# Weights' low parts kept in DRAM between token blocks, and a memset between GpSimd's scatters

## The chip, the cores and the metric

One core of one Trainium2 chip runs the whole program. The metric is the device time of one execution in microseconds (us), lower is better; the number shown is the median over runs.

## The reference

One layer of a streaming encoder on 1024 tokens of 1024 channels, all in float32:

```python
n = modulate(rms_norm(h, g_norm1[l]), shift1, scale1)
p = n @ w_in[l]
a_val, a_gate, u, v, gate_a, gate_b = jnp.split(p, splits, axis=-1)
y_a = conv_branch(a_val, a_gate, ...)          # GLU, causal depthwise conv of width 31, LayerNorm, silu, @ w_conv_out
y_b = sgu_branch(u, v, ...)                    # LayerNorm, masked 128x128 mixing per group, @ w_sgu_out
merged = jax.nn.sigmoid(gate_a) * y_a + jax.nn.sigmoid(gate_b) * y_b
h = h + gate1[:, None, :] * (merged @ w_out[l])

n2 = modulate(rms_norm(h, g_norm2[l]), shift2, scale2)
h = h + gate2[:, None, :] * peer(n2, w_query[l], sub_keys[l], expert_u[l], expert_v[l])
return rms_norm(h, g_final)
```

`peer` is a retrieval: for each token and each of 8 heads the scores against 2 x 128 keys, the 16 best pairs, and a softmax over them, which gives 128 experts of 16384 with a gate each. An expert is one row of `expert_u` (dot product with the token, gelu, times the gate) and one row of `expert_v` (added with that factor).

## The kernel before, in words

The work has two parts, the front (everything up to the scores and the choice of experts) and the dense stage (the experts).

The front takes the tokens in three blocks of 3, 2 and 3 tiles of 128 tokens (`BLOCKS`). Each block multiplies the same 88 weight tiles of 128x1024: 8 each of `w_v`, `w_av`, `w_ag`, `w_u`, `w_gb`, `w_sgu`, `w_ga`, `w_conv`, `w_out`, and 16 of `w_q`; `w_v`, `w_av` and `w_ag` of the next block come while the present block does `w_q`. A float32 product is made of three faster ones (`mm3`): weights and inputs are each split into a high part, a rounded copy (`whi`, by ScalarE, line 203), and a low part, the difference (`wlo`, by VectorE, line 161). `fetch_w` loads the next raw tile (two buffers), `split_w` starts the split as a task, `next_w` hands out a finished pair and starts another, so two pairs are under way ahead of the one in use.

The order of all instructions on each engine is laid down when the program is built, by a planner (`Plan`) that adds up assumed costs and gives background work its turn: routing and convolution first, then the rest. Loads and most stores go through SyncE's queue (SP) in program order; a transfer at its head that waits holds up those behind it.

Routing (`route`, on VectorE) chooses the experts of one tile after another. What follows depends on the tile. For tiles 0 to 2 the gates are added into an array `g_a` in DRAM, which was filled with zeros at the start: per tile 128 indirect DMAs issued by GpSimd (`scatter`, line 573), each with one gate for each of the 128 tokens, at the places that a tile `at` names (line 1234). The 16 of a head wait for those of the head before. For tiles 3 and 4 the gates are expanded by one-hot products (`Scatter`): VectorE makes `o1`, `o2` and `so`, PE multiplies, ScalarE gathers 32 tokens in four `st` tiles (`evacuate`) and these are stored to `g_b`. For tiles 5 to 7 the numbers of the experts are stored.

The last block's last two scores are stored by GpSimd (`store` with `late`), behind what GpSimd has in its queue. `fence`, a memset of one column on GpSimd, waits for all scatters; the loads of the gates from `g_a` wait for the fence. The dense stage then runs all experts over tiles 0 to 4 on PE (`u_piece`, `v_unit`) with these gates, while GpSimd gathers single experts' rows for tiles 5 to 7 (line 1396) and VectorE multiplies them.

Of the kernel before, what the change touches and what calls it, by code (L numbers as in the profile page):

```python
# [7 lines left out]
F32 = mybir.dt.float32  # L8
F32R = mybir.dt.float32r
# [7 lines left out]
P = 128  # L17
D = 1024
# [14 lines left out]
TC = 32  # L33
NCH = NB // TC
ZW, ZN = 128, 16
NST = 5
NRAW = 2
NSO = 2
NPG = 3
# [262 lines left out]
def build(ctx, tc, I, O):  # L302
    nc = tc.nc
    out = O["out"]
    pl = Plan(nc)
    ctx.enter_context(tc.manual_schedule())

    dram = ctx.enter_context(tc.tile_pool(name="dram", bufs=1, space=bass.MemoryType.DRAM))
# [6 lines left out]
    g_a = dram.tile([NCA, P, P * TC], F32, name="g_a")  # L315
    g_b = dram.tile([NCH - NCA, P, P * TC], F32, name="g_b")
    g_1 = g_a.rearrange("c p (x o) -> (c p x) o", o=1)
    e_d = dram.tile([NA, P, P], I32, name="e_d")
    ga_d = dram.tile([NA, P, P], F32, name="ga_d")

    cst = ctx.enter_context(tc.tile_pool(name="cst", bufs=1))
# [126 lines left out]
    class Scatter:  # L448
# [50 lines left out]
        def produce(self):  # L499
            n, last = 0, None  # L500
            while n < NOH * self.NQ or last:
                if last:
                    while len(self.so) > 1:
                        yield pl.now + 0.2
                    r = yield from self.scaled(*last)
                    self.so.append(r)
                    last = None
                    if n % self.NQ == 0:
                        self.tiles.pop(0)
                if self.tiles:  # L510
                    last = yield from self.onehots(n)
                    n += 1
                    self.made = n
                else:
                    yield pl.now + 0.3
# [32 lines left out]

    SYNC = mybir.DependencyInfo(mybir.DependencyClass.Sync, mybir.DependencyReason.DATA)
    zeroed, heads = [], []  # L550

    def zeros(zt):

# [8 lines left out]
    def scatter(gate, at):  # L562


        while not zeroed:
            yield pl.now + 2.0
        yield max(pl.ready(at), pl.ready(gate))
        before = []
        for h in range(H):
            now = []  # L570
            for k in range(h * K, (h + 1) * K):
                nc.gpsimd.nop()
                i = nc.gpsimd.indirect_dma_start(  # L573
                    out=g_1, out_offset=bass.IndirectOffsetOnAxis(ap=at[:, k:k + 1], axis=0),
                    in_=gate[:, k:k + 1], in_offset=None, compute_op=OP.add).ins
                tc.declare_no_dep(i, group="sc", keep=before, reason="other tokens, or other experts")
                for o in before:
                    tc.add_manual_dep(i, o.name, SYNC, reason="sums of gates")
                tc.add_to_no_dep_group("sc", i)
                pl.op("pool", 2.0, [], [gate, at])  # L580
                now.append(i)
            before = now
            yield max(pl.now, pl.t["pool"] - 30.0)
        heads.append(before)
# [32 lines left out]
    def flat(w):  # L617
        return w.rearrange("p j c -> p (j c)")

    def weights():  # L620
        def w_v():
            for cb in range(2):
                for jq in range(4):
                    yield flat(I["w_v"][cb, jq])

        yield from w_v()
        for b in range(len(BLOCKS)):
            for j in range(J):
                if b == 0:
                    yield flat(I["w_av"][j])  # L630
                    yield flat(I["w_ag"][j])
                yield flat(I["w_u"][j])
            for j in range(J):
                yield flat(I["w_gb"][j])
                yield flat(I["w_sgu"][j])
            for n in ("w_ga", "w_conv"):
                for j in range(J):
                    yield flat(I[n][j])
            for cb in range(2):
                for jq in range(4):  # L640
                    yield flat(I["w_out"][cb, jq])
            if b + 1 < len(BLOCKS):
                yield from w_v()
            for j in range(J):
                if b + 1 < len(BLOCKS):
                    yield flat(I["w_av"][j])
                    yield flat(I["w_ag"][j])
                yield flat(I["w_q"][2 * j])
                yield flat(I["w_q"][2 * j + 1])

    wsrc = weights()
    raws, ahead = [], []

    def fetch_w():
        src = next(wsrc, None)
        if src is not None:
            raws.append(wp.tile([P, D], F32, name="raw", tag="raw", bufs=2))
            pl.load(raws[-1], src)

    def split_w():  # L660
        if raws:
            hi = wp.tile([P, D], F32R, name="whi", tag="whi", bufs=3)
            lo = wp.tile([P, D], F32R, name="wlo", tag="wlo", bufs=3)
            raw = raws.pop(0)

            def work():
                yield from pl.split(hi, lo, raw)
                fetch_w()

            ahead.append((hi, lo, pl.task(work())))  # L670
            ahead[-1][2][3] = -1
# [1023 lines left out]
```

## Time and profile before

| | |
|---|---|
| median of 3 runs | 3475.64 us (3469.93 to 3485.93) |
| profiled execution | 3466.49 us, of which the span is 3464.4 |
| granted TensorE clock, mean | 0.946 |
| PE busy | 3094.6 us (89%) |
| VectorE (DVE) busy | 2999.9 us (87%) |
| ScalarE (ACT) busy | 1142.6 us (33%) |
| GpSimd (POOL) busy | 1683.9 us (49%) |

The span runs from the first to the last instruction of the profiled execution. Busy times are sums over stages that differ: in the front (about the first 1500 us) and in the dense stage (from about 1640 us) other engines can set the pace, so the stages are to be read one by one.

### The profile page before, as it was taken

The numbers are of one execution on the slowest core, as the hardware profiler recorded it, in microseconds if no ns is written. First come the engines' busy times: TensorE is split into PE (matmuls) and PEld (weight loads), VectorE is DVE, ScalarE is ACT, GpSimd is POOL, SyncE is SP. The second block draws the span as 40 slices with busy tenths as digits, with TensorE's granted clock in tenths as the row PEclk, the third lists the DMA queues.
The fourth block names the chain that finished last, engine by engine and source line by source line (L and its number), as shares of the span: only waits on it lengthen the run. The fifth ranks groups of instructions, "written<-read, shape, count | busy, mean of one in ns | idle before, by whom it ended". The sixth has DMA issues, their size and how long they took to land.

```text
span 3464.4 us, 48530 instructions
## 1 busy us (share of the span) xinstructions
PE 3094.6 (89%) x17598; PEld 2811.1 (81%) x17598; DVE 2999.9 (87%) x5922; ACT 1142.6 (33%) x1964; POOL 1683.9 (49%) x1165
## 2 busy tenths in 40 slices
PE   7978969977989978954999999999999999999991
PEld 4977848966889967954999998888899998999991
DVE  3898768988999987745999998999999998999998
ACT  4324434435442335631322222222222223222221
POOL 0000000037788888883222555666665554655664
PEclk9989979998999988977999999999999999999995
DMA  5965655546655547653766899999999998999997
GB/s 190 278 208 164 214 180 171 171 125 153 162 127 122 122 89 179 160 144 81 235 217 216 305 353 331 363 333 370 341 357 346 349 347 304 357 346 361 341 347 287
DMA packets 434721, 852.71 MB, mean 246 GB/s; under 512 B 83272, under 2 KB 242888, under 8 KB 434480
## 3 DMA queue, kind: packets, MB, share of 16 engines
q1 hardware_dynamic: 268464, 446.28, 38.3%
q0 software_dynamic: 166016, 403.32, 36.5%
q8 instruction: 138, 2.26, 0.3%
q14 instruction: 103, 0.84, 0.1%
HBM read 785.94 MB, written 63.52 MB: 245 GB/s over the span
## 4 chain that ended last, share of the span: by engine, by line
PE 34%; DVE 27%; DMA 14%; POOL 12%; issue 9%; ACT 2%; SPq 0%; DVEq 0%; POOLq 0%; ACTq 0%
PE pa L144 13%; POOL g_a L573 10%; PE ps L144 9%; PE pk L144 7%; PE pr L144 5%; DMA w<-in_v,e 4%; DVE wlo L161 4%; DVE ya L174 4%; DMA raw<-in_v 4%; DVE zc L174 3%; DVE odd L174 3%; DVE scr L174 2%; POOL w L1396 1%; DMA w<-in_u,e 1%; DVE yb L161 1%
## 5 line engine op out<-in xcount | busy, mean ns | idle before, releaser
L573 POOL DMA_INDIRECT g_a<-gate,at x384 | 706.7, 1840 | 883.4 <-DVE at L168 744.2
L1396 POOL DMA_INDIRECT w<-in_u,e x384 | 483.2, 1258 | 541.6 <-DVE scr L174 367.8
L144 PE MATMUL pa<-n2h,uh 128*128 128x320 f32 x2016 | 624.9, 310 | 82.2 <-ACT ge L195 75.1
L1396 POOL DMA_INDIRECT w<-in_v,e x384 | 489.7, 1275 | 336.8 <-DVE ya L174 238.0
L144 PE MATMUL pa<-n2l,uh 128*128 128x320 f32 x2016 | 625.6, 310 | 0.2 <-DVE n2l L161 0.2
L144 PE MATMUL pa<-n2h,ul 128*128 128x320 f32 x2016 | 625.0, 310 | 0.0
L174 DVE SCALAR_TENSOR_TENSOR ya<-w,aa,ya 128x1024 f32<-128x1024 f32 x381 | 488.9, 1283 | 23.8 <-DMA w<-in_v,e 19.1
L174 DVE SCALAR_TENSOR_TENSOR scr<-w,n 128x1024 bf16<-128x1024 f32 x384 | 469.1, 1222 | 10.2 <-DMA w<-in_u,e 4.8
L144 PEld LDWEIGHTS pa<-n2h,uh 128*128 128x128 f32 x2016 | 380.5, 189 | 94.4 <-ACT ge L195 77.9
L203 ACT CAST whi<-raw 128x1024 fp32r<-128x1024 f32 x264 | 276.4, 1048 | 370.3 <-PE ps L144 100.9
L144 PEld LDWEIGHTS pa<-n2l,uh 128*128 128x128 f32 x2016 | 380.1, 189 | 10.9 <-DVE n2l L161 1.1
L161 DVE TENSOR_TENSOR wlo<-raw,whi 128x1024 fp32r<-128x1024 f32 x264 | 320.9, 1219 | 75.1 <-ACT whi L203 73.1
L144 PE MATMUL ps<-nh,whi 128*128 128x384 f32 (+1 forms) x1024 | 355.9, 348 | 31.5 <-DVE z L161 17.5
L144 PEld LDWEIGHTS pa<-n2h,ul 128*128 128x128 f32 x2016 | 380.5, 189 | 0.0
L144 PE MATMUL ps<-nh,wlo 128*128 128x384 f32 (+1 forms) x1024 | 345.8, 338 | 21.9 <-DVE wlo L161 21.8
L144 PE MATMUL ps<-nl,whi 128*128 128x384 f32 (+1 forms) x1024 | 344.7, 337 | 1.6 <-DVE nl L161 1.6
L195 ACT ACTIVATE ge<-pa 128x320 f32<-128x320 f32 x249 | 108.5, 436 | 693.6 <-PE pa L144 693.6
L144 PE MATMUL pk<-vh,hh 128*128 128x512 f32 x768 | 299.5, 390 | 0.0
L144 PE MATMUL pk<-vl,hh 128*128 128x512 f32 x768 | 299.5, 390 | 0.0
L144 PE MATMUL pk<-vh,hl 128*128 128x512 f32 x768 | 299.3, 390 | 0.0
L203 ACT CAST hh<-ge 128x320 fp32r<-128x320 f32 x250 | 115.0, 460 | 526.5 <-DVE ge L161 526.5
L144 PE MATMUL ps<-gh,whi 128*128 128x256 f32 (+1 forms) x704 | 218.3, 310 | 20.3 <-ACT gh L203 18.4
(251 smaller groups left out, 6538.3 us busy)
## 6 DMA issues: line engine op xcount, KB each, us to landing
raw<-in_uT SPq DMA_DIRECT2D x128, 512.0 KB, 6.6
raw<-in_v SPq DMA_DIRECT2D x128, 512.0 KB, 7.3
g_a<-zt SPq DMA_DIRECT2D x24, 1024.0 KB, 6.9
raw<-in_w_q SPq DMA_DIRECT2D x48, 512.0 KB, 3.9
gt<-g_a SPq DMA_DIRECT2D x32, 640.0 KB, 14.6
aw<-in_w_ada SPq DMA_DIRECT2D x32, 512.0 KB, 7.3
g_b<-st SPq DMA_DIRECT2D x32, 512.0 KB, 4.1
gt<-g_b SPq DMA_DIRECT2D x32, 512.0 KB, 12.5
```

The costliest lines, as they stand in the source:

```text
L144: self.nc.tensor.matmul(ps, w, x, start=start, stop=stop)
L161: self.nc.vector.tensor_tensor(out=out, in0=a, in1=b, op=op)
L174: self.nc.vector.scalar_tensor_tensor(out, a, s, b, op0=op0, op1=op1, **kw)
L195: self.nc.scalar.activation(out, a, func, **kw)
L203: self.nc.scalar.copy(out, a)
L573: i = nc.gpsimd.indirect_dma_start(out=g_1, out_offset=bass.IndirectOffsetOnAxis(ap=at[:, k:k + 1], axis=0), in_=gate[:, k:k + 1], in_offs ...
L1396: nc.gpsimd.indirect_dma_start(out=w, out_offset=None, in_=I["v" if ph else "u"], in_offset=bass.IndirectOffsetOnAxis(ap=ra[a][0][:, k:k + ...
```

## The change

Three things change. First, when block 0 has split a weight tile, its low part is also stored to a DRAM tile of its own (`lo_d`); when a later block comes to a tile that has one, the low part is loaded (`fetch_lo`, one tile ahead) and VectorE's subtraction is left out. The high part is still copied from the raw tile. `wlo` gets a fourth buffer. Second, space for it is taken from `st`: four buffers instead of five, and `produce` makes the next `so` when none is waiting instead of at most one. Third, between two scatters GpSimd runs a memset of one column of a tile `pad` in place of a nop, and the planner counts 1.9 us for a scatter instead of 2.0.

```diff
--- before.py
+++ after.py
@@ -33,7 +33,7 @@
 TC = 32
 NCH = NB // TC
 ZW, ZN = 128, 16
-NST = 5
+NST = 4
 NRAW = 2
 NSO = 2
 NPG = 3
@@ -315,6 +315,7 @@
     g_a = dram.tile([NCA, P, P * TC], F32, name="g_a")
     g_b = dram.tile([NCH - NCA, P, P * TC], F32, name="g_b")
     g_1 = g_a.rearrange("c p (x o) -> (c p x) o", o=1)
+    lo_d = {}
     e_d = dram.tile([NA, P, P], I32, name="e_d")
     ga_d = dram.tile([NA, P, P], F32, name="ga_d")
 
@@ -500,7 +501,7 @@
             n, last = 0, None
             while n < NOH * self.NQ or last:
                 if last:
-                    while len(self.so) > 1:
+                    while self.so:
                         yield pl.now + 0.2
                     r = yield from self.scaled(*last)
                     self.so.append(r)
@@ -548,6 +549,7 @@
 
     SYNC = mybir.DependencyInfo(mybir.DependencyClass.Sync, mybir.DependencyReason.DATA)
     zeroed, heads = [], []
+    pad = cst.tile([P, 1], F32, name="pad")
 
     def zeros(zt):
 
@@ -569,7 +571,7 @@
         for h in range(H):
             now = []
             for k in range(h * K, (h + 1) * K):
-                nc.gpsimd.nop()
+                nc.gpsimd.memset(pad, 0.0)
                 i = nc.gpsimd.indirect_dma_start(
                     out=g_1, out_offset=bass.IndirectOffsetOnAxis(ap=at[:, k:k + 1], axis=0),
                     in_=gate[:, k:k + 1], in_offset=None, compute_op=OP.add).ins
@@ -577,7 +579,7 @@
                 for o in before:
                     tc.add_manual_dep(i, o.name, SYNC, reason="sums of gates")
                 tc.add_to_no_dep_group("sc", i)
-                pl.op("pool", 2.0, [], [gate, at])
+                pl.op("pool", 1.9, [], [gate, at])
                 now.append(i)
             before = now
             yield max(pl.now, pl.t["pool"] - 30.0)
@@ -621,51 +623,69 @@
         def w_v():
             for cb in range(2):
                 for jq in range(4):
-                    yield flat(I["w_v"][cb, jq])
+                    yield "w_v", (cb, jq)
 
         yield from w_v()
         for b in range(len(BLOCKS)):
             for j in range(J):
                 if b == 0:
-                    yield flat(I["w_av"][j])
-                    yield flat(I["w_ag"][j])
-                yield flat(I["w_u"][j])
+                    yield "w_av", (j)
+                    yield "w_ag", (j)
+                yield "w_u", (j)
             for j in range(J):
-                yield flat(I["w_gb"][j])
-                yield flat(I["w_sgu"][j])
+                yield "w_gb", (j)
+                yield "w_sgu", (j)
             for n in ("w_ga", "w_conv"):
                 for j in range(J):
-                    yield flat(I[n][j])
+                    yield n, (j)
             for cb in range(2):
                 for jq in range(4):
-                    yield flat(I["w_out"][cb, jq])
+                    yield "w_out", (cb, jq)
             if b + 1 < len(BLOCKS):
                 yield from w_v()
             for j in range(J):
                 if b + 1 < len(BLOCKS):
-                    yield flat(I["w_av"][j])
-                    yield flat(I["w_ag"][j])
-                yield flat(I["w_q"][2 * j])
-                yield flat(I["w_q"][2 * j + 1])
+                    yield "w_av", (j)
+                    yield "w_ag", (j)
+                yield "w_q", (2 * j)
+                yield "w_q", (2 * j + 1)
 
     wsrc = weights()
-    raws, ahead = [], []
+    raws, ahead, los = [], [], {}
 
     def fetch_w():
-        src = next(wsrc, None)
-        if src is not None:
-            raws.append(wp.tile([P, D], F32, name="raw", tag="raw", bufs=2))
-            pl.load(raws[-1], src)
+        k = next(wsrc, None)
+        if k is not None:
+            raws.append((k, wp.tile([P, D], F32, name="raw", tag="raw", bufs=2)))
+            pl.load(raws[-1][1], flat(I[k[0]][k[1]]))
+
+    def fetch_lo():
+
+        if raws and raws[0][0] in lo_d:
+            k = raws[0][0]
+            los[k] = wp.tile([P, D], F32R, name="wlo", tag="wlo", bufs=4)
+            pl.load(los[k].bitcast(F32), lo_d[k])
 
     def split_w():
         if raws:
             hi = wp.tile([P, D], F32R, name="whi", tag="whi", bufs=3)
-            lo = wp.tile([P, D], F32R, name="wlo", tag="wlo", bufs=3)
-            raw = raws.pop(0)
+            k, raw = raws.pop(0)
+            old = k in los
+            lo = los.pop(k) if old else wp.tile([P, D], F32R, name="wlo", tag="wlo", bufs=4)
 
             def work():
+                if old:
+                    yield pl.ready(raw)
+                    f = pl.acopy(hi, raw)
+                    fetch_w()
+                    fetch_lo()
+                    yield max(f, pl.ready(lo))
+                    return
                 yield from pl.split(hi, lo, raw)
                 fetch_w()
+                lo_d[k] = dram.tile([P, D], F32, name="lo_d_%s_%s" % (k[0], str(k[1]).strip("()").replace(", ", "_")))
+                pl.load(lo_d[k], lo.bitcast(F32))
+                fetch_lo()
 
             ahead.append((hi, lo, pl.task(work())))
             ahead[-1][2][3] = -1
```

## Rows read from the trace of the kernel before

**Rows 1.** The page of the profiled execution: busy time, share and instructions of each engine, and then the span in 40 slices of 86.6 us, each digit the busy share in tenths.

```profile
PE 3094.6 (89%) x17598; PEld 2811.1 (81%) x17598; DVE 2999.9 (87%) x5922; ACT 1142.6 (33%) x1964; POOL 1683.9 (49%) x1165
...
PE   7978969977989978954999999999999999999991
...
POOL 0000000037788888883222555666665554655664
```

**Rows 2.** The page's chain of work that ended last: its share of the span by line.

```profile
PE pa L144 13%; POOL g_a L573 10%; PE ps L144 9%; PE pk L144 7%; PE pr L144 5%; DMA w<-in_v,e 4%; DVE wlo L161 4%; DVE ya L174 4%; DMA raw<-in_v 4%; DVE zc L174 3%; DVE odd L174 3%; DVE scr L174 2%; POOL w L1396 1%; DMA w<-in_u,e 1%; DVE yb L161 1%
```

**Rows 3.** The chain of waits between 1400 and 1660 us, all engines: engine, line, whom it waited for, us in total, times, longest.

```profile
ACT vh L203 <- DMA sc_d<-so: 72.3, 1, 72.3
...
PE pa L144 <- ACT ge L195: 71.8, 1, 71.8
```

**Rows 4.** The waits of SyncE's DMA queue between 1480 and 1660 us, same columns.

```profile
SPq L236 <- DVE vals L355: 78.3, 4, 71.7
```

**Rows 5.** The timeline of GpSimd from 1586 to 1600 us: start, us, engine, line, operation, and in brackets the idle time before it.

```profile
1591.62 1.55 POOL L573 DMA_INDIRECT g_a<-gate,at  x1 [0.30 <-issue]
1592.60 2.23 POOL L229 DMA_DIRECT2D sc_d<-so  x2
1594.79 0.16 POOL L589 MEMSET fence<- 128x1 f32 x1
```

**Rows 6.** The waits of GpSimd over 600 to 1800 us.

```profile
POOL g_a L573 <- DVE at L168: 744.2, 1, 744.2
POOL g_a L573 <- issue: 113.6, 373, 0.3
...
POOL g_a L573 <- DMA g_a<-gate,at: 24.9, 8, 6.4
```

**Rows 7.** The instructions that write or read the tile at (the scatters' places) between 600 and 1100 us: count, duration in ns (smallest, median, largest), first and last start.

```profile
L573 POOL DMA_INDIRECT g_a<-gate,at x149: 1544/1569/9207, 747.3 to 1099.7; - x149
L168 DVE TENSOR_SCALAR at<-i1f,tok x3: 286/286/286, 746.7 to 1029.2; 128x128 int32<-128x128 f32 x3
```

**Rows 8.** GpSimd's scatters as one group, first in 747 to 1532 us and then in 1532 to 1600 us (two answers): count, busy us and mean ns of one, idle time before them and who ended it.

```profile
L573 POOL DMA_INDIRECT g_a<-gate,at x352 | 657.0, 1866 | 869.1 <-DVE at L168 744.2 <-issue 104.5 <-DMA g_a<-gate,at 19.8
...
L573 POOL DMA_INDIRECT g_a<-gate,at x32 | 49.8, 1555 | 14.2 <-issue 9.1 <-DMA g_a<-gate,at 5.1
```

**Rows 9.** GpSimd's timeline from 800 to 812 us, a scatter over a subtraction.

```profile
801.23 1.56 POOL L573 DMA_INDIRECT g_a<-gate,at  x1 [0.31 <-issue]
803.09 2.78 POOL L573 DMA_INDIRECT g_a<-gate,at  x1 [0.30 <-issue]
```

**Rows 10.** VectorE's timeline in the same place.

```profile
803.22 1.22 DVE L161 TENSOR_TENSOR wlo<-raw,whi 128x1024 fp32r<-128x1024 f32 x1
```

**Rows 11.** Busy time by stretch. Columns: stretch, its length, PE, PEld, DVE, ACT, POOL busy us with counts, granted clock, DMA share, GB/s.

```profile
87.00:174.00 87.00, 84.82 (x500) 84.18 (x499) 74.87 (x137) 28.96 (x37) 0.00 (x0) 1.00 0.91 278
...
478.00:642.00 164.00, 152.21 (x972) 145.11 (x971) 138.07 (x318) 71.34 (x121) 0.00 (x0) 0.98 0.55 182
642.00:747.00 105.00, 95.67 (x775) 92.88 (x774) 96.06 (x282) 40.66 (x59) 0.00 (x0) 1.00 0.50 158
747.00:1500.00 753.00, 654.51 (x3869) 597.63 (x3868) 656.81 (x1781) 344.94 (x688) 632.35 (x337) 0.92 0.59 138
1500.00:1593.00 93.00, 20.68 (x122) 18.32 (x119) 20.08 (x65) 14.32 (x32) 74.20 (x49) 0.61 0.43 84
...
1641.00:3464.00 1823.00, 1741.77 (x9733) 1581.84 (x9731) 1695.20 (x2696) 479.24 (x782) 972.95 (x768) 0.98 0.91 324
```

**Rows 12.** All instructions that write or read the tile wlo: count, duration in ns (smallest, median, largest), first and last start.

```profile
L161 DVE TENSOR_TENSOR wlo<-raw,whi x264: 1203/1219/1273, 42.9 to 1471.4; 128x1024 fp32r<-128x1024 f32 x132
```

**Rows 13.** Busy time by stretch of the instructions that write or read the tile wlo alone: stretch, length, PE, PEld, DVE busy us with counts, granted clock, DMA share, GB/s.

```profile
87.00:174.00 87.00, 51.52 (x154) 28.76 (x153) 23.19 (x19) 1.00 0.91 278
478.00:642.00 164.00, 88.62 (x277) 53.02 (x277) 46.27 (x38) 0.98 0.55 182
642.00:747.00 105.00, 67.03 (x237) 44.41 (x237) 35.30 (x29) 1.00 0.50 158
747.00:1500.00 753.00, 309.68 (x908) 176.28 (x908) 146.79 (x121) 0.92 0.59 138
```

**Rows 14.** VectorE's costliest groups between 747 and 1500 us.

```profile
L161 DVE TENSOR_TENSOR wlo<-raw,whi 128x1024 fp32r<-128x1024 f32 x121 | 146.8, 1218 | 16.0 <-ACT whi L203 15.6
L174 DVE SCALAR_TENSOR_TENSOR zc<-z,cw,zc 128x384 f32<-128x384 f32 (+1 forms) x117 | 69.6, 595 | 0.0
L174 DVE SCALAR_TENSOR_TENSOR odd<-z,cw,odd 128x384 f32<-128x384 f32 (+1 forms) x108 | 64.3, 595 | 0.0
L161 DVE TENSOR_TENSOR so<-o,gB 128x1536 bf16<-128x1536 bf16 x62 | 59.0, 951 | 0.0
```

**Rows 15.** GpSimd's timeline among the first gathers, same columns as in rows 5.

```profile
1677.07 0.95 POOL L1396 DMA_INDIRECT w<-in_u,e  x1 [0.30 <-issue]
```

**Rows 16.** The instructions on the tile st that moves the expanded gates to g_b: its stores, and the idle time that ended with their landing (us, times).

```profile
L236 SPq DMA_DIRECT2D g_b<-st x32: 319/410/2236, 1366.1 to 1519.7; - x32
...
  DMA g_b<-st: 21.6, 15
```

**Rows 17.** The instructions that write the tile so, the gates' expansions (other uses of the name are left out), same columns.

```profile
L161 DVE TENSOR_TENSOR so<-o,gB x64: 944/951/998, 1339.4 to 1503.3; 128x1536 bf16<-128x1536 bf16 x64
```

**Rows 18.** The page's DMA issues: out and in, queue, count, KB each, median us from issue to landing.

```profile
g_b<-st SPq DMA_DIRECT2D x32, 512.0 KB, 4.1
```

## Prediction

> **What bounds the kernel now.** The page comes first. PE is busy 89% of the span, but the slices show a hole: slices 18 and 19 have PE at 5 and 4 tenths between slices at 9, and there GpSimd (POOL), idle for the first eight slices, is at 8 and 3 [rows 1]. The chain that ended last puts 10% of the span, some 350 us, on GpSimd's scatters of line 573, more than on any weight product of the front [rows 2]. The waits around the hole tell why. PE waited 71.8 us in one piece, and ScalarE 72.3 us for one transfer, the last scores stored from `so` [rows 3]; SyncE's queue stood 71.7 us in one piece behind a load of scores [rows 4]. That store is issued on GpSimd, behind all the scatters: the last scatter starts at 1591.62, the two stores at 1592.60, the fence at 1594.79 [rows 5]. So the dense stage starts when the scatters end, not when the front's products end.
>
> What sets the scatters' end is GpSimd itself. Once started it waited for nothing but 24.9 us of its own landings; the rest of its idle time is 0.3 us before each instruction [rows 6]. So the end is start + 384 periods. The start is `at` of the first tile, at 746.7 us [rows 7], made by VectorE. The period has two levels: 352 scatters up to 1532 us take a mean of 1.866 us, and the last 32, when VectorE is nearly idle, 1.555 us [rows 8], each after 0.30 us. The difference, 352 x 0.311 = 109 us, is time in which a scatter is held by VectorE: in one place a scatter of 2.78 us, 1.22 longer than its neighbour, began at 803.09 [rows 9] and a subtraction of 1.22 us ran from 803.22 [rows 10]. After the fence the dense stage runs 1823 us with PE busy 1742 of them [rows 11]; the change has no instruction there.
>
> **What the change removes.** 264 subtractions `wlo` of 1.219 us [rows 12] split the weights, 88 in each block. With the low parts kept, the 176 of blocks 1 and 2 go: 215 us of VectorE. This is not the gain, for VectorE isn't the bound. It counts in two places.
>
> The start. In 478 to 642 us VectorE is busy 138 of 164 us and in 642 to 747 us 96 of 105 [rows 11]; there run 38 and 29 subtractions, 46.3 and 35.3 us [rows 13]. Of the first 38 the 16 of `w_q` remain, so 22 go, 27 us; all 29 of the second go. That is 62 us of work ahead of `at` on a nearly full engine. The routing of the first tile shares VectorE with the convolution in turns, which may take what is freed: between 0 and 62 I take half, 30 us earlier.
>
> The holding. In 747 to 1500 us the subtractions are 146.8 us, the two convolution groups 133.9, the expansion `so` 59.0 [rows 14], all with two inputs in SBUF. The subtractions' share is 147/340 = 43%, and of 109 us that is 47. The work left moves together and holds a little more, so I take 40, with 15 to 57 as bounds (57 if the expansion holds nothing, 15 if most of the freed time fills with convolution).
>
> **What it adds.** 88 stores and 176 loads of 512 KB on SyncE's queue. The dense stage moves 324 GB/s at a share of 0.91 [rows 11], 356 GB/s when busy, so one costs 524 KB/356 = 1.47 us of the DMA engines. In blocks 1 and 2 the share is 0.59 [rows 11], and 176 x 1.47 = 259 us goes into about 0.41 x 858 = 350 free ones: covered, if evenly spread; each load then queues on SyncE until the product three before is done, which delays other loads by a few us, but not the scatters. Block 0 is tighter. In 87 to 174 us the share is 0.91 and 278 GB/s [rows 11], with 19 subtractions [rows 13], so 19 stores: 28 us of transfers into 8 free. Up to 20 us of delay; part lands on the zeroing of `g_a`, due only at 747, so I take 15, between 0 and 20. The store waits for the subtraction that the next raw load waits for anyway, so it adds no wait of its own to the queue, while in blocks 1 and 2 the raw buffer is free already after ScalarE's copy.
>
> The Trainium skill, DMA: Bandwidth & Descriptors, section Specifications, gives about 358 GB/s of HBM per core. By it that stretch would need 278 + 19 x 524 KB/87 us = 393 GB/s and last 10% longer, 8 us instead of the 20 of the rows; our 356 is near it.
>
> The memset. The nop has no row: POOL's 1165 instructions [rows 1] are 768 gathers, 384 scatters and 13 more. So 384 memsets are new work on the engine that sets the end. No row has a memset between two scatters. From above: the fence, a memset of the same 128x1, took 0.16 us [rows 5] after the store's end; in series that is 61 us. From below: the 0.30 us before each scatter and each gather [rows 8, 15] may be lost only between two indirect DMAs; the plain store behind the last scatter began 0.98 us after it, before its end [rows 5]. If the memset fills the gap and ends it, 384 x 0.30 = 115 us go. Neither row is nearer, so I take the middle, (-115 + 61)/2 = -27 us.
>
> The Trainium skill, GPSIMD Engine Reference, section 2.1 Instruction dispatch, says that a core of GpSimd goes on to the next instruction as soon as its own share is done. By it the memset would overlap the scatter's tail and cost nothing, so -55 us in all instead of -82; no run shows it yet.
>
> The buffers. With four `st` instead of five each chunk of 32 tokens must wait for its own four stores, and the expansion makes one `so` ahead instead of two. There are eight chunks: ScalarE waited 21.6 us in all for `g_b` stores, the last of which starts at 1519.7 [rows 16], the 64 expansions run from 1339.4 to 1503.3 [rows 17], one per 2.56 us. Seven waits of at most the median landing, 4.1 us [rows 18], and some for the queue: 30 to 60 us more on that loop. It is covered today by 1593 - 1520 = 73 us, and it begins earlier as VectorE is freed, so nothing; without the cover it is the third rival below.
>
> **The sum.** Start -30 + 15, holding -40, memset -27: -82 us. The profiled execution took 3466.5 us (span 3464.4 and 2.1 around it), so 3384; it lies 9 us below the median of the three runs, 3475.6. On the median's scale I write **3390**. The measurement tells about 0.5%, 17 us.
>
> **The rivals.**
> (a) The memset only ends the gap: start and holding as above, -55 - 115 = -170, so 3296. But the front then becomes the bound: PE is busy 655 of 753 us between 747 and 1500 [rows 11], so its end can't move more than 15 + 98; the floor is about 3466 - 130 = 3336. For it: every gap is the same 0.30. Against: the first scatter, behind no other, came 0.3 us after `at` ended too (746.7 + 0.286 to 747.3) [rows 7].
> (b) The memset runs in series: -55 + 61 = +6, 3472, no change. For it: GpSimd takes its instructions in order.
> (c) The expansion into `g_b` ends last: if it takes 60 us longer and begins only 30 earlier, its end goes from 1520 to 1550, 43 us before today's end: 3423.
> (d) The change does half of it: a weight whose predecessor is still being split when it is taken gets no stored low part and is subtracted again. If half do: start 15 - 15, holding -20, memset -27: 3420.
> (e) Slower: the stores in block 0 are paid in full, each ahead of the next raw load on one queue, 88 x 1.47 = 129 us. Then the start moves +129 - 30, with holding and memset -67: +32, 3498. It decides the sign once block 0 loses more than 97 us. For it: the raw loads stand behind the stores. Against: the DMA share is 0.55 in 478 to 642 us [rows 11], so nearly half is free there.
>
> **Chances.** Forecast 0.47; (a) 0.12; (c) 0.09; (d) 0.09; (b) 0.13; (e) 0.10. Faster by over 0.5% holds the forecast, (a), (c) and (d): 0.77; within 0.5% (b): 0.13; slower (e): 0.10. The forecast's own range, with the memset half way to either bound (44 us), is 3346 to 3434. For 8 in 10 I leave out (e) and the lower half of (a): 3330 to 3475.
>
> **What would show it.** Right: 88 `wlo` subtractions left; `at` of the first tile near 730; the first 352 scatters near 1.75 us; scatters' end near 1510, and PE idle longer than 72 us before it, as the front ends earlier still. The start-to-start spacing of the last, undisturbed scatters gives the memset's price: 1.86 now, 1.79 forecast, 2.02 for (b), 1.56 for (a). Wrong: the chain before the dense stage on `g_b` or on weight products, or a block 0 whose products wait for `raw`.

## The result, and the profile after

The changed kernel took 3423.62 us, median of 4 runs (3423.22 to 3424.94), against 3473.8 us before in 4 runs beside it: a ratio of 0.985, 95% interval 0.9826 to 0.9875 (here and below the ratio is estimated from the single runs, so it can differ a little from that of the two medians). That is 50 us where 82 to 84 were forecast. The span of the profiled execution went from 3464.4 to 3421.1 us, 43 less; the profiled execution of before lies 7 us under its median, which is why the two differences differ. The mean granted clock went from 0.946 to 0.956.

The page of after: busy time and the slices, each digit the busy share in tenths [rows 1], and the chain that ended last by line [rows 2].

```profile
span 3421.1 us, 49027 instructions
...
PE 3086.7 (90%) x17598; PEld 2810.1 (82%) x17598; DVE 2804.2 (82%) x5741; ACT 1148.2 (34%) x1978; POOL 1674.1 (49%) x1549
...
PE   7969859888999969878999999999999999999991
...
POOL 0000000027899999981232556566665554565663
...
PE ps L144 12%; POOL g_a L575 12%; PE pa L144 12%; PE pk L144 7%; DVE ya L174 6%; DMA raw<-in_v 5%; PE pr L144 5%; DMA w<-in_v,e 3%; DVE scr L174 2%; DVE yb L161 1%; DVE zc L174 1%; DVE vl L161 1%; DVE wlo L161 1%; DVE odd L174 1%; POOL w L1416 1%
```

VectorE lost 196 us of work, yet the scatters still lead the chain into the dense stage. The hole in PE's slices, 5 and 4 tenths before, is now at 7 and 8.

Next the scatters and memsets as groups (500 to 1700 us), the tile `at`, and the end of GpSimd's timeline; these answer to [rows 5, 7, 8].

```profile
L575 POOL DMA_INDIRECT g_a<-gate,at x384 | 654.9, 1705 | 842.3 <-DVE at L168 747.2 <-issue 70.0 <-DMA g_a<-gate,at 24.8
L574 POOL MEMSET pad<- 128x1 f32 x383 | 274.2, 716 | 0.0
```

```profile
L168 DVE TENSOR_SCALAR at<-i1f,tok x3: 288/288/336, 749.7 to 911.5; 128x128 int32<-128x128 f32 x3
```

```profile
1542.71 1.56 POOL L575 DMA_INDIRECT g_a<-gate,at  x1 [0.19 <-issue]
1543.68 0.71 POOL L574 MEMSET pad<- 128x1 f32 x1
1544.58 1.56 POOL L575 DMA_INDIRECT g_a<-gate,at  x1 [0.19 <-issue]
1545.55 2.25 POOL L229 DMA_DIRECT2D sc_d<-so  x2
1547.69 0.22 POOL L591 MEMSET fence<- 128x1 f32 x1
```

Over the same stretch the 384 scatters of before had a mean of 1840 ns. So the 43.3 us of the span fall into three pieces. The scatters start 3.0 us later (`at` of the first tile 749.7 instead of 746.7). From the first scatter to the last it takes 794 us instead of 844, 50 less, and the fence comes at 1547.7 instead of 1594.8, 47 earlier. From the fence to the end it takes 1873 us instead of 1870, 4 more.

The scatters' 50 us split in two. All 384 means against an undisturbed scatter give the holding: before (1.840 - 1.555) x 384 = 109 us, after (1.705 - 1.56) x 384 = 56 us, 53 less. The start-to-start spacing of undisturbed scatters went from 1.86 to 1.87 us, which is 4 us more on 384.

Windows of after (columns as in [rows 11]); the one line of before for 260 to 350 us stands first, since [rows 11] leaves it out.

```profile
260.00:350.00 90.00, 75.94 (x387) 69.69 (x386) 77.22 (x127) 38.83 (x58) 0.00 (x0) 0.92 0.48 157
```

```profile
87.00:174.00 87.00, 80.94 (x460) 79.64 (x459) 68.23 (x125) 25.95 (x33) 0.00 (x0) 0.96 0.92 314
260.00:350.00 90.00, 86.91 (x464) 80.05 (x463) 82.93 (x133) 32.84 (x47) 0.00 (x0) 1.00 1.04 353
478.00:642.00 164.00, 140.68 (x856) 132.78 (x855) 115.09 (x278) 68.11 (x118) 0.00 (x0) 0.94 0.79 276
642.00:747.00 105.00, 87.75 (x635) 84.93 (x634) 79.02 (x311) 35.53 (x57) 0.00 (x0) 0.95 0.75 266
747.00:1500.00 753.00, 668.37 (x4149) 617.98 (x4148) 522.57 (x1695) 368.38 (x732) 664.40 (x726) 0.95 0.84 242
```

VectorE is 23 us less busy in 478 to 642 us, 17 less in 642 to 747 and 134 less in 747 to 1500. The DMA engines carry more: in 260 to 350 us their share went from 0.48 to 1.04, in 478 to 642 us from 0.55 to 0.79.

The waits of all engines between 1400 and 1640 us [rows 3], and the longest of SyncE's queue there [rows 4]:

```profile
ACT vh L203 <- DMA sc_d<-so: 30.5, 1, 30.5
...
PE pa L144 <- ACT ge L195: 29.7, 1, 29.7
```

```profile
SPq L236 <- DMA sc_d<-so: 58.2, 8, 36.7
```

The same wait for the last scores is still there, but it fell from 71.8 to 29.7 us: the scatters end 47 us earlier, while the front's last store of scores on SyncE starts at 1504.7, 5 us later than the 1499.3 of before. 71.8 - 47.1 + 5.4 gives 30. The stores of scores on SyncE from 1400 us on, of before and then of after:

```profile
L236 SPq DMA_DIRECT2D sc_d<-so x9: 370/371/1564, 1407.6 to 1499.3; - x9
```

```profile
L236 SPq DMA_DIRECT2D sc_d<-so x14: 360/424/863, 1439.2 to 1504.7; - x14
```

In after, the tile wlo, and then the expansions `so` and the stores of `st`:

```profile
L161 DVE TENSOR_TENSOR wlo<-raw,whi x90: 1204/1221/1228, 42.3 to 842.1; 128x1024 fp32r<-128x1024 f32 x90
...
L236 SPq DMA_DIRECT2D wlo<-lo_d_w_q x32: 320/387/1230, 902.2 to 1491.7; - x32
```

```profile
L161 DVE TENSOR_TENSOR so<-o,gB x64: 946/952/1005, 1184.0 to 1400.0; 128x1536 bf16<-128x1536 bf16 x64
```

```profile
L236 SPq DMA_DIRECT2D g_b<-st x32: 319/422/1172, 1255.3 to 1406.0; - x32
```

90 subtractions are left, two above the 88 of block 0. The expansions [rows 17] take 216 us instead of 164, but begin 155 us earlier.

The loads of `w_q` in block 0 show how far that block is behind, first in the kernel before and then in the one after:

```profile
L236 SPq DMA_DIRECT2D raw<-in_w_q x16: 327/328/731, 493.8 to 622.4; - x16
```

```profile
L236 SPq DMA_DIRECT2D raw<-in_w_q x16: 328/336/1388, 502.2 to 642.7; - x16
```

### The profile page after: what moved, and what is told of

It reads as the page before. It is cut to its first block, busy times and chain, and to the rows that moved or that the text cites. A ratio compares the mean times of both kernels' runs of the same rounds, so it can differ in the third digit from the quotient of the medians.

```text
span 3421.1 us, 49027 instructions
## 1 busy us (share of the span) xinstructions
PE 3086.7 (90%) x17598; PEld 2810.1 (82%) x17598; DVE 2804.2 (82%) x5741; ACT 1148.2 (34%) x1978; POOL 1674.1 (49%) x1549
## 4 chain that ended last, share of the span: by engine, by line
PE 36%; DVE 19%; DMA 18%; POOL 14%; issue 9%; ACT 3%; SPq 1%; DVEq 0%; ACTq 0%; POOLq 0%
PE ps L144 12%; POOL g_a L575 12%; PE pa L144 12%; PE pk L144 7%; DVE ya L174 6%; DMA raw<-in_v 5%; PE pr L144 5%; DMA w<-in_v,e 3%; DVE scr L174 2%; DVE yb L161 1%; DVE zc L174 1%; DVE vl L161 1%; DVE wlo L161 1%; DVE odd L174 1%; POOL w L1416 1%
## 5 line engine op out<-in xcount | busy, mean ns | idle before, releaser
L575 POOL DMA_INDIRECT g_a<-gate,at x384 | 654.9, 1705 | 842.3 <-DVE at L168 747.2
L574 POOL MEMSET pad<- 128x1 f32 x384 | 274.3, 714 | 0.0
```

Source lines behind the costliest of these rows:

```text
L574: nc.gpsimd.memset(pad, 0.0)
L575: i = nc.gpsimd.indirect_dma_start(out=g_1, out_offset=bass.IndirectOffsetOnAxis(ap=at[:, k:k + 1], axis=0), in_=gate[:, k:k + 1], in_offs ...
```

## The experiments

The theory from the forecast: the two-input instructions of VectorE hold the scatters; the stores of block 0 cost time ahead of `at`; the memset's price is open; the smaller buffers are covered. The main rival for the gain was that VectorE's load as such, or the moved DMA traffic, sets the scatters' pace.

**The memset: three runs.** On the kernel before, put in alone:

```diff
+    pad = cst.tile([P, 1], F32, name="pad")
...
-                nc.gpsimd.nop()
+                nc.gpsimd.memset(pad, 0.0)
```

> The kernel before with one edit: a memset of one column in place of the nop between two scatters. Theory H (the 50 us come from scatters that are held less, and the memset lies under the tail of the scatter before it): no change, 3474 us within 10, undisturbed spacing 1.86 to 1.87 us, mean spacing 2.20 as before. Theory M (the memset itself shortens the holding, for instance because it takes the shared port before VectorE's next instruction): 25 to 50 us faster, the six scatters over 4 us and the many of 2 to 3 us fewer, mean spacing near 2.1.

Measured: 3475.67 us against 3471.67, ratio 1.0001 (0.9982 to 1.002). The scatters' group:

```profile
L574 POOL DMA_INDIRECT g_a<-gate,at x384 | 708.1, 1844 | 840.0 <-DVE at L168 748.7 <-issue 68.7 <-DMA g_a<-gate,at 22.2
```

A mean of 1844 ns against 1840, and the holding as before. So the memset alone gave none of the gain, and on the kernel before it took nothing that can be measured. (The planner's 1.9 us for a scatter was not run by itself.)

The other way round, on the changed kernel, the nop in its place, run on two chips, on the second beside the changed kernel itself once more (without an edit):

```diff
-                nc.gpsimd.memset(pad, 0.0)
+                nc.gpsimd.nop()
```

> The changed kernel with the nop back in place of the memset. Theory H: as the changed kernel, 3424 us within 10, the gap before each scatter 0.30 us again and the spacing the same. Theory M: 25 to 50 us slower than the changed kernel, 3449 to 3474.

> The changed kernel with the nop, once more. If the memset costs what its run suggested (undisturbed spacing 1.87 against 1.86 us, and a scatter run 6 us shorter), 5 to 14 us faster than the changed kernel beside it, intervals apart; if that was the chip, within 4 us of it.

> The changed kernel once more, beside the next three on one chip: 3424 us within 8.

Measured: without it 3412.88 us, ratio 0.9815 (0.9794 to 0.9836), and 3416.89, ratio 0.9834 (0.9818 to 0.985); the changed kernel again 3422.27, ratio 0.9849 (0.9833 to 0.9864). The last scatters without the memset:

```profile
1537.75 1.55 POOL L575 DMA_INDIRECT g_a<-gate,at  x1 [0.30 <-issue]
1539.61 1.55 POOL L575 DMA_INDIRECT g_a<-gate,at  x1 [0.30 <-issue]
```

The spacing is 1.86 us here and 1.87 with the memset. Both comparisons, the first of them by way of the kernel before, lean the same way, 0.15 to 0.35% or 5 to 12 us, but their intervals overlap, those of the pair run side by side too: the memset costs between nothing and that.

**The stores alone.** All low parts are stored, none is loaded, every block subtracts:

```diff
-        if raws and raws[0][0] in lo_d:
+        if False:
```

> The changed kernel with the low parts stored each time a weight is split but never loaded: all 264 subtractions stay, and as every block splits, every block stores (264 stores, no loads). Theory H with a price for the stores: the places of the first tile are ready 20 to 60 us later than before (767 to 807 us, because the subtractions ahead of it stay and the stores of block 0 are paid), the scatters are held as before, so 3490 to 3530 us. Rival F (the stores are hidden and the routing just did not use the freed time): places ready at 747 to 755 us and 3474 us within 15.

Measured: 3522.38 us, ratio 1.0139 (1.012 to 1.0158). Here blocks 1 and 2 store too, so the whole time says little; the places of the first tile and the stretches ahead of them belong for the most part to block 0:

```profile
L168 DVE TENSOR_SCALAR at<-i1f,tok x3: 286/287/288, 779.4 to 1060.6; 128x128 int32<-128x128 f32 x3
```

```profile
260.00:350.00 90.00, 86.97 (x471) 81.50 (x470) 84.97 (x137) 31.98 (x46) 0.00 (x0) 1.00 1.04 352
478.00:642.00 164.00, 145.26 (x881) 135.93 (x880) 124.27 (x263) 69.23 (x121) 0.00 (x0) 0.92 0.79 260
```

779.4 - 746.7 = 33 us is the price of the stores ahead of the first tile's places. Not all of it is block 0's: the stores of block 1 for `w_v`, `w_av`, `w_ag` and `w_u`, 32 of them, start before 700 us. From there to the changed kernel's 749.7 it is 30 us back, which is the relief of VectorE if block 1's loads in the changed kernel cost what its stores cost here. The mean scatter is 1826 ns, near before's 1840: stores alone do not release the scatters. The whole time is long for another reason too: the expansion ends last here, its last `g_b` store starts at 1647.7, behind the last scatter at 1628.6.

**Two inputs or one.** The changed kernel with its stores and loads, but wherever a low part was loaded VectorE does a useless instruction over the raw tile: in one run a subtraction with two inputs into the raw tile, in the other a MAX8 with one input and 8 results.

```diff
-                    f = pl.acopy(hi, raw)
+                    yield pl.acopy(hi, raw)
+                    f = pl.sub(raw, raw, hi.bitcast(F32))
```

```diff
+    scrap = fc.tile([P, 8], F32, name="scrap")
...
-                    f = pl.acopy(hi, raw)
+                    yield pl.acopy(hi, raw)
+                    nc.vector.max(out=scrap, in_=raw)
+                    f = pl._v([scrap], [raw], D)
```

> The changed kernel, low parts stored and loaded as there, but where a low part is loaded VectorE makes the subtraction all the same, raw minus high part, into the raw tile, and nothing reads it: the DMA traffic of after with VectorE's work of before. Theory H (scatters are held by VectorE instructions with two inputs in SBUF): the scatters are held some 100 us in all instead of 54, mean spacing 2.18 to 2.21, scatters last 835 to 850 us instead of 794, places of the first tile 20 to 30 us later; over 3490 us. Rival T (the 50 us come from the DMA side, a scatter's end or its landing being nearer): holding stays at 54 us.

> The same with a maximum over the raw tile in place of the subtraction: one input in SBUF, eight values out, about the same time on VectorE (estimate 1.1 us from the subtraction's 1.22). Theory H: holding stays near 54 us and the scatters last 790 to 805 us, though VectorE is as busy as in the kernel before; only the start is later. Rival B (any busy VectorE holds the scatters): holding near 100 us as with two inputs.

Measured: 3539.0 us, ratio 1.0179 (1.0158 to 1.0199), and 3471.36, ratio 0.9984 (0.9973 to 0.9994). For each run first VectorE's added instructions in 747 to 1500 us and then the scatters' group; the run with two inputs comes first.

```profile
L161 DVE TENSOR_TENSOR raw<-raw,whi 128x1024 f32<-128x1024 f32 x130 | 158.2, 1220 | 37.9 <-ACT whi L203 37.8
```

```profile
L575 POOL DMA_INDIRECT g_a<-gate,at x384 | 701.5, 1827 | 881.0 <-DVE at L168 785.4 <-issue 69.8 <-DMA g_a<-gate,at 25.6
```

```profile
L681 DVE MAX8 scrap<-raw 128x8 f32<-128x1024 f32 x127 | 154.8, 1219 | 5.5 <-DMA raw<-in_w_out 5.0 <-DMA raw<-in_w_conv 0.2
```

```profile
L575 POOL DMA_INDIRECT g_a<-gate,at x384 | 660.2, 1719 | 876.9 <-DMA wlo<-lo_d_w_ga 775.9 <-issue 69.6 <-DMA g_a<-gate,at 31.2
```

The added instructions are nearly equal in number and length (158 and 155 us), and VectorE is as busy in that stretch as before the change, 649 and 662 us against 657. The holding is (1.827 - 1.56) x 384 = 103 us with two inputs and (1.719 - 1.56) x 384 = 61 us with one, against 109 before and 56 after. The scatters singly say the same: of those from 740 to 1500 us, the 107 whose first 1.56 us lie for over 0.5 us beside a MAX8 take a mean of 1.62 us, the 107 that lie so beside the added subtraction 1.92 us. A busy VectorE does not hold a scatter; the subtraction does. The two instructions differ in their output as well, 128x1024 against 128x8, and these runs do not tell the second input from the wide result. The Trainium skill, SBUF — State Buffer, section Who interferes with whom, says that a VectorE instruction with two inputs in SBUF contends with a GpSimd instruction that reads SBUF, and one with a single input, outside the two-port modes, does not; 103 and 61 us agree with it, if issuing a scatter reads SBUF, which no run here tests. The same section tells of a probe in which `tensor_tensor`, the kind of the subtraction, did not stall a DMA; here it held the issue of indirect ones.

These two runs also bear on the start and the front. In the one with one input the traffic is that of the changed kernel and VectorE is about as busy as before; the places, the expansions and the front's last stores of scores are:

```profile
L168 DVE TENSOR_SCALAR at<-i1f,tok x3: 289/334/370, 778.4 to 1046.2; 128x128 int32<-128x128 f32 x3
```

```profile
L161 DVE TENSOR_TENSOR so<-o,gB x64: 941/952/997, 1360.8 to 1527.4; 128x1536 bf16<-128x1536 bf16 x64
```

```profile
L236 SPq DMA_DIRECT2D sc_d<-so x12: 370/371/385, 1402.1 to 1523.5; - x12
```

With the added traffic and about the same work on VectorE, the places come 32 us later than before (778.4 for 746.7) and the front's last store 24 us later (1523.5 for 1499.3); freeing VectorE brings 29 and 19 us back (749.7 and 1504.7), and lets the expansions begin 177 us earlier (1184.0). With two inputs the places come at 787.9, which reads 41 and 38 us. That run, like the stores alone, is long also because the expansion ends last (its last `g_b` store at 1660.6, the last scatter at 1629.6).

**The buffers alone,** on the kernel before:

```diff
-NST = 5
+NST = 4
...
-                    while len(self.so) > 1:
+                    while self.so:
```

> The kernel before with four st buffers instead of five and the next so made only when none waits. Forecast: the expansion loop takes 0 to 60 us longer (164 us before from first to last so), still ends before the scatters, 3474 us within 10. Rival: it becomes the last to end, or moves work of VectorE so that scatters are held otherwise; then over 17 us either way.

Measured: 3487.07 us, ratio 1.0047 (1.0029 to 1.0066), some 16 us slower and outside the 10 that were expected.

```profile
L161 DVE TENSOR_TENSOR so<-o,gB x64: 945/951/1004, 1338.6 to 1605.3; 128x1536 bf16<-128x1536 bf16 x64
```

```profile
L236 SPq DMA_DIRECT2D g_b<-st x32: 319/458/2802, 1363.9 to 1611.6; - x32
```

The loop takes 267 us instead of 164, and its last store starts at 1611.6, behind the last scatter at 1589: without the rest of the change the expansion ends last. The length does not hang on the buffers alone: with the same four, and VectorE filled by MAX8, the loop took 167 us.

**The zeros spread out.** `g_a` is filled with zeros while block 0 runs. To take them out of the stores' way, the planner leaves 20 us instead of 4 between two fills:

```diff
-                yield pl.now + 4.0
+                yield pl.now + 20.0
```

> The changed kernel with the 24 zero fills of block 0 spread out: 20 us of the planner between two instead of 4. Theory S (the stores cost the start because they meet the zero fills at a DMA share near 1): weight tiles of block 0 land earlier, places of the first tile 8 to 20 us earlier (730 to 742), 3404 to 3416 us. Rival R (the same bytes have to move before 747 us in any case): places at 745 to 755 and 3424 us within 8.

Measured: 3487.51 us, ratio 1.003 (1.0016 to 1.0043), outside what either theory had. The fills (tile `zt`), and the places (tile `at`):

```profile
L236 SPq DMA_DIRECT2D g_a<-zt x24: 378/434/1351, 89.7 to 801.3; - x24
```

```profile
L168 DVE TENSOR_SCALAR at<-i1f,tok x3: 286/286/288, 779.4 to 952.6; 128x128 int32<-128x128 f32 x3
```

The last fill starts at 801.3, and the first scatter only at 811.7. But the places are late too, 779.4 instead of 749.7. The first load of `w_gb` comes 6 us earlier than in the changed kernel (198.0 for 204.4), the first of `w_q` 16 us later (518.4 for 502.2) and the last of `w_q` in block 0 30 us later (672.2 for 642.7): the fills cost more among the later loads than they saved among the early ones. The run did not show a cheaper place for the zeros.

**The early weights stored later.** The changed kernel, but `w_v`, `w_av`, `w_ag` and `w_u` are stored only the second time they are split:

```diff
-    raws, ahead, los = [], [], {}
+    raws, ahead, los, once = [], [], {}, set()
...
+                if k[0] in ("w_v", "w_av", "w_ag", "w_u") and k not in once:
+                    once.add(k)
+                    fetch_lo()
+                    return
```

> The changed kernel with the low parts of w_v, w_av, w_ag and w_u not stored in block 0 but in block 1, where they are split once more (32 subtractions back, 39 us). Theory S2 (the price of the stores falls in the first 190 us, where the DMA share is above 0.9): block 0 is back in time by then, w_gb starts near 193 us as before instead of 204, but the 32 subtractions come back ahead of the first tile's places: places at 745 to 765, scatters held some 10 us more, 3424 to 3440 us. Rival (the price falls later, between 260 and 650 us): w_gb near 193 us too, places at 765 to 785, over 3440 us.

Measured: 3406.31 us, ratio 0.9804 (0.9788 to 0.9819), better than was expected. The places and the zero fills of this run, and under them the fills of the kernels before and after:

```profile
L168 DVE TENSOR_SCALAR at<-i1f,tok x3: 286/286/286, 734.9 to 904.3; 128x128 int32<-128x128 f32 x3
```

```profile
L236 SPq DMA_DIRECT2D g_a<-zt x24: 377/432/797, 91.4 to 316.9; - x24
```

```profile
L236 SPq DMA_DIRECT2D g_a<-zt x24: 381/432/891, 90.4 to 284.8; - x24
```

```profile
L236 SPq DMA_DIRECT2D g_a<-zt x24: 377/515/1176, 90.3 to 390.8; - x24
```

The 32 stores move from the first split to the second, 24 of them into the stretch of `w_q` at the end of block 0, and 31 subtractions come back: yet the places come 15 us earlier than in the changed kernel, and the fence at 1529.2 comes 18.5 us earlier. The run is 16 us faster than the changed kernel beside it. So most of the gain is the start. Where the price of the other transfers arises can be read from `w_q`: its first load comes at 489.8, 12 us earlier than in the changed kernel, but from the first load to the last in block 0 it takes 140 us, as in the changed kernel (140.5) and not as before (128.6). This run settles one more thing, by the stores of scores on SyncE and PE's longest wait:

```profile
L236 SPq DMA_DIRECT2D sc_d<-so x13: 359/386/881, 1402.7 to 1465.2; - x13
```

```profile
PE pa L144 <- ACT ge L195: 51.0, 1, 51.0
```

The front's last store is 39.5 us earlier here than in the changed kernel, but the time follows the fence and not the front, and PE waits 51 us: the scatters' end, with the store behind it, still sets where the dense stage starts.

**One tile fewer to scatter.** `NDD`, the number of tiles whose gates are scattered, 2 instead of 3, the third being expanded like the others:

```diff
-NDD = 3
+NDD = 2
```

> The changed kernel with two tiles scattered by GpSimd and three expanded by one-hot products (NDD 2 for 3). If the scatters alone set the start of the dense stage, their 256 end near 1290 us and more than 60 us go. Theory P (behind the scatters stands PE's front, whose last scores are out at 1505 us in the changed kernel): the front now ends last, and the third expansion adds 32 groups of products to it, so the dense stage starts between 1510 and 1560; 3390 to 3440 us.

Measured: 3420.12 us, ratio 0.9825 (0.9803 to 0.9847). GpSimd's timeline around the end of its scatters:

```profile
1345.71 1.56 POOL L575 DMA_INDIRECT g_a<-gate,at  x1 [0.19 <-issue]
1531.24 1.64 POOL L229 DMA_DIRECT2D sc_d<-so  x2 [183.97 <-ACT so L203]
1532.87 0.12 POOL L591 MEMSET fence<- 128x1 f32 x1
```

With the scatters done 199 us earlier GpSimd waits 184 us for the front's last scores, and the time hardly moves. Next behind the scatters stands the front's own end, 1526 us in this run (the last store of scores on SyncE; 1505 in the changed kernel, which expands a tile less).

**The last scores on SyncE.** The changed kernel with the nop, and the last block's last two scores stored by SyncE instead of GpSimd behind the scatters:

```diff
-                nc.gpsimd.memset(pad, 0.0)
+                nc.gpsimd.nop()
...
-        pl.late = not nxt
+        pl.late = False
```

> The changed kernel with the nop and with the last scores stored by SyncE instead of by GpSimd behind the scatters. Theory Q (PE's last 30 us of waiting before the dense stage come from these stores, not from the gates' array): the splits of the first dense rows go on before the scatters end, the dense stage starts 10 to 25 us earlier, 3388 to 3403 us. Rival G (the fence and the load of the gates behind it set the start anyway): 3413 us within 6.

Measured: 3397.82 us, ratio 0.9768 (0.9753 to 0.9784), 19 us below the run with the nop alone beside it, with intervals apart. The stores of scores from 1400 us on, and the longest wait of PE in 1400 to 1640 us:

```profile
L236 SPq DMA_DIRECT2D sc_d<-so x16: 359/382/800, 1432.5 to 1506.1; - x16
```

```profile
PE ps L154 <- ACT sga L195: 7.9, 1, 7.9
```

The 29.7 us wait of PE is gone: the last scores no longer stand behind the scatters. It is the fastest of all versions run. Its combination with the later stores of the early weights was not tried.

## Why the prediction was right and wrong

The sign and the mechanism held: fewer two-input subtractions, shorter scatters, an earlier fence. The sum did not: -82 forecast, -43 in the span. That the time still lies inside the forecast's own range of 3346 to 3434 is in part luck: the range was that wide for the memset's sake, and 13 us more from the holding made up for part of what the start (18 us) and the memset (31 us) fell short.

**The holding** was forecast at -40 with bounds 15 to 57; it was -53, near the upper bound. The two-input and one-input runs put it to the subtractions. The freed time did not fill with convolution: its two groups took 122.6 us in 747 to 1500 us against 133.9 [rows 14]. The scatters' mean over the first 352 came to 1.715 us, below the 1.75 forecast.

**The start** is the first step that failed: -30 + 15 was written, and about -30 + 33 happened (-30 + 33 by the run with the stores alone, -29 + 32 by the run with MAX8; the run with two inputs reads -38 + 41). The relief was about right. The price of the added traffic was mis-sized, beyond even the bound of 20. The working looked for a full stretch, found the one of 87 to 174 us, priced its 19 stores and let the other 69 pass as covered by an average share of 0.5. The loads show otherwise. The first load of `w_gb` came 11 us later than before (204.4 for 193.4), the first of `w_out` 16.5, the first of `w_q` only 8, the last of `w_q` in block 0 again 20 (642.7 for 622.4). So a second part of the price arose in 502 to 643 us, at a share that went from 0.55 to 0.79 in 478 to 642 us. There the 16 stores of `w_q` meet the first low parts that are loaded for block 1, and the working called those loads covered. Which of the two costs the time is not shown: in the run with the early weights stored later both kinds are stores, and the stretch is as long.

And the zeros, which the working took as free until 747 us, were moved: the last fill went from 284.8 to 390.8 us and kept the engines full, 353 GB/s at 1.04, in 260 to 350 us where a share of 0.48 had been. The Trainium skill (DMA: Bandwidth & Descriptors, Specifications) has about 358 GB/s as the limit, and 353 lies just under it; but a slice of the dense stage of before reached 370 GB/s, so no run here shows 358 to be a ceiling, and the 8 us worked out by it were no better than the 20.

**The memset** is the second: -27 was the middle of -115 and +61, and the measured spacing is 0.01 us longer, 4 us in all. Neither bounding row was the mechanism. The memset starts 0.97 us after its scatter and ends before the next could have begun. The row nearest to it was there: the plain store that began 0.98 us after the last scatter, before its end [rows 5]. Weighed as the rule of overlap, it gives zero; the prediction named it only as a reason for the gain. The Trainium skill's rule (GPSIMD Engine Reference, 2.1 Instruction dispatch), by which the memset costs nothing, agrees with the rows. The sum of -55 that went with it lies near the -47 at the fence only because start and holding missed in opposite directions.

**The buffers** came out at nothing, as forecast, but not for the reason given. The cover of 73 us would not have held: on the kernel before the loop grew by 103 us and ended last. In the changed kernel it grew by 52 us, and what covered it was that it began 155 us earlier, where 30 had been allowed in rival (c). That this comes of the freed VectorE is shown by the run with MAX8, where the expansions begin at 1360.8, later than before.

**The front** did not end earlier, so PE's wait shrank instead of growing. Its last scores came 5 us later: by the run with MAX8 the traffic cost its end 24 us, and the freed VectorE gave 19 back. The forecast had the second, and of the first only a few us. Which transfers cost it most was not isolated; with the early weights stored later the front's last store came 39.5 us earlier. As long as the front ends where it does in the changed kernel, the 30 us that PE still waits are about what the scatters have left to give; the run with two scattered tiles agrees, though its front has more to expand.

Of the rivals none occurred: no gap closed (a), no memset in series (b), the last `g_b` store starts at 1406.0 and far ahead of the last scatter (c), 90 subtractions left (d), a start moved by some 33 us and not 129 (e). Rivals (c) and (d) gave 3423 and 3420, almost the measured number, by mechanisms that are not there. With the terms as measured, the working gives -30 + 33 - 53 + 4 = -46 to the fence, where -47 was seen; the dense stage took 4 back.

Two slips changed nothing. In rival (a) 15 + 98 is 113 and gives a floor of 3353, not 3336. And the 71.7 us of SyncE's queue were not spent on a load of scores: the transfer that started when the wait ended, at 1599.17, loads a tile of the dense stage, as its timeline shows:

```profile
1599.17 0.33 SPq L236 DMA_DIRECT2D raw<-in_v  x1
```

## What to carry to other kernels

When work is traded for traffic, price each transfer in the stretch in which it runs, and ask what it pushes on: a low-priority transfer that is moved into the next stretch fills that one too. An instruction put between two others of an in-order engine is priced by whether it may start before the first has ended; look in the trace for any pair of unlike instructions there. And ask what stands just behind the bound: here PE's wait of 72 us, not the 109 us of holding, was the most that faster scatters could win while the front ended where it did, and moving the last stores off the bound's queue was worth 19 us.

## What was not expected of the hardware

A memset of 0.71 us between two scatters lengthened their spacing by 0.01 us: it lies under the tail of the scatter (1.56 us long, next instruction at 0.97). Why two scatters alone stand 1.86 us apart, with 0.30 us idle, stays open. A VectorE instruction of 1.22 us held scatters with two inputs and a wide result, and hardly at all with one input and 8 results (103 and 61 us of holding in all, 56 without either). And the fullest stretch of the front that was read shows a DMA share above 1.0, at 353 GB/s.
